# A list schedule that charges a change of tile shape on the tensor engine and keeps to the shape at hand for a while

## The chip, the cores and the metric

One core of one Trainium2 chip runs the whole program. The engines that matter are PE (TensorE, matrix products), ACT (ScalarE), DVE (VectorE), POOL (GpSimd) and SP, whose queue issues the DMAs that bring weights from DRAM to the on-chip SBUF. Products accumulate in eight PSUM banks. The metric is device time in microseconds (us), lower is better.

## The reference

256 tokens of 1024 features go through three residual blocks, each a mixer and a feed-forward part with layer norms:

```python
x = layer_norm(ALPHA * x + mix, ...)                 # layer 0: NSA attention + pooling
x = layer_norm(ALPHA * x + sqrelu_mlp(x, w1, w2))    # 1024 -> 4096 -> 1024
...                                                  # layer 1: gated linear attention, the same MLP
# block 2: mixer = gated delta rule (8 heads of 128, chunks of 64) + spatial gating unit,
#          then a hierarchical mixture of 16 experts (4 groups of 4, width 256, top 2 in the group)
a_mat = tril(k_beta @ k.T * decay, -1) + eye         # one 64x64 matrix for each chunk and head
u, w  = solve(a_mat, v_beta), solve(a_mat, k_beta * exp(g_cum))
for chunk in chunks:                                 # 4 of them, one after the other
    v_new = u - w @ state
    out   = q_dec @ state + qk @ v_new
    state = state * g_last + k_dec.T @ v_new
```

All inputs and the output are float32. The products need more than float16 accuracy.

## The kernel before

A weight arrives as float32 by DMA and is split into two float16 parts, the high part on ACT and the rest on DVE. A large product is then three float16 products (high by high, high by low, low by high). Nearly all the work on PE is of this kind: a 128x128 stationary tile (128 rows, 128 columns) and 256 or 512 moving columns. These are called dense here.

The delta rule (`mixer`, L1306) is different. For each token tile `solve` (L1371) inverts the 64x64 matrices of four heads and two chunks by doubling: `quads` (L1376) issues a batch of 8 float32 products with 64x64 stationary tiles in two corners of the array, five levels one after the other, with a DVE subtraction, an ACT copy and a POOL product between (L1443 to L1456). `own` (L1382) and `recur` (L1464) are further batches with 128x64, 64x64 or 64x128 stationary tiles. This chain has long waits in it, and the dense products of the same block that do not depend on it (projections, the spatial gating unit, the gates `pg`, the products `psu` and `py`) fill them. When the chain is done, `to_xt` (L740) transposes its result with the identity (`ptr`, 16 transposes of 128x128 in four groups, one group for each half of a token tile); ACT and DVE split each group into two float16 parts (L736), and the last `py` products (weight w_dn_out) use them. Then follow w_out, the router, and the experts: tokens are gathered with products of dense shape, and the up products of the experts have 128x64 stationary tiles (`peg`).

What sets the order is the class `Plan`. Every instruction is recorded with its inputs (`add`, L182) and a planned duration (`_cost`, L153). `order` (L228) then runs a list schedule: when an engine comes free in planned time, it takes the ready instruction with the lowest number in the program whose tiles have a place (L423 to L438). Results reach another engine after a planned delay. For PE two rules come first: if its recent activity is low, a large product is preferred (L405 to L414), and if the next product in the program uses other columns of the array, it goes along with the first (L415 to L421). Where PE has nothing to do, a filler goes out: a product of the constant k_ones with itself, to keep PE active (L484 to L497, issued at L546). The result is one fixed instruction list for each engine, issued at L551, so almost every row of the profile bears that line. On the chip every engine works through its list in order, and an instruction waits for its inputs. The planned durations decide the order only. SP's list of DMAs is in the same plan: a load goes out when the SBUF block that it fills has been released by its last reader.

In the order rows below, P_110 to P_117 are PSUM banks, H_n are blocks of the SBUF heap, and k_... are constants.

Of the kernel before, what the change touches and what calls it, by code (L numbers as in the profile page):

```python
# [8 lines left out]
F32 = mybir.dt.float32  # L9
# [15 lines left out]
class Plan:  # L25
    """Records engine instructions in program order and issues them in the order of a
    list schedule: per engine, the earliest recorded instruction whose inputs and tile
    slots are available goes first. Tiles of one tag take their slots in program order."""
# [8 lines left out]
    # the tensor engine runs at half its clock after a tick with less work than BUSY (ns at the full clock)  # L37
    TICK, BUSY = 10240 / 3, 1280.0

    # function tables of the scalar engine: those that hold a function, and what a change costs  # L40
    TABLES = {AF.Exp: (0,), AF.Tanh: (0, 10), AF.Gelu: (10,), AF.Ln: (5,)}
    LOAD = 1283.0

# [11 lines left out]
    def __init__(self, nc):  # L55
# [17 lines left out]
        self.low = 0.0  # L73
        self.keep, self.calm, self.leak, self.cap = None, 100.0, 0.55, 350.0
# [8 lines left out]
    def tile(self, shape, name, dtype, tag, slots, psum=False, lead=None):  # L83
        """slots: a count, or the numbers of the slots that the tile may take; None for a tile in the heap,
        in blocks of 1, 2 or 4 KB per partition. lead: a kind of tile that is filled well ahead of its use, while
        fewer of the kind than its quota are in the heap; kinds of one line take their places in program order."""
# [4 lines left out]
        if slots is None:  # L91
            self.units[handle.name] = next(k for k in (1, 2, 4) if size <= 1024 * k)
            slots = 0
# [9 lines left out]
    def branch(self, flag, bound, body):  # L103
        """The body runs if the integer in flag is above bound."""
        self.flags.append((flag, bound))
        self.segment += 1
        body()
        self.segment += 1
# [34 lines left out]
    @staticmethod  # L143
    def _run(ap, first):
        """Bytes of the longest run of consecutive addresses, the dimensions before first left out."""
        n = 1
        for step, count in reversed([d for d in ap.ap[first:] if d[1] > 1]):
            if step != n:
                break
            n *= count  # L150
        return n * mybir.dt.size(ap.dtype)
# [30 lines left out]
    def add(self, eng, method, fn, args, kwargs):  # L182
# [36 lines left out]
        cols = 0  # L219
        if eng == "PE":  # L220
            p0 = outs[0].offset // outs[0].ap[0][0]
            cols = sum(1 << b for b in range(p0 // 32, -(-(p0 + outs[0].ap[0][1]) // 32)))
# [3 lines left out]
                         eng == "PE" and ins[0].dtype == F32, table, self.urgent))  # L226

    def order(self):  # L228
# [50 lines left out]
        issued, warm, prior = 0, 0, -1  # L279
        since = level = last = 0.0  # L280
# [19 lines left out]
        def fit(t):  # L300
# [24 lines left out]
            if b > cur:  # L325
                # what the program needs from here to there, one instruction after the other, has to fit beside it
# [11 lines left out]
            # the place in the block that leaves the larger piece whole  # L338
# [46 lines left out]
        while issued < n:  # L385
# [10 lines left out]
            while moved:  # L396
                moved = False
                for e in ready:
# [16 lines left out]
                    if e == "PE" and pick is None and prior >= 0 and ops[prior + 1:prior + 2]:  # L415
                        # the second of two products in different columns of the array runs along with the first
# [5 lines left out]
                    late = None  # L422
                    while pick is None and ready[e] and len(skipped) < 48:  # L423
# [26 lines left out]
                    if e == "PE":  # L450
                        c = ops[pick][11]
                        prior = pick
                        clock()
                        if c & array:
# [6 lines left out]
                        if not fast:  # L461
                            dur *= 2
                    self.began[pick] = now
# [20 lines left out]
            if self.keep and busy["PE"] <= now and pe_left[seg] and seg % 2 == 0 and any(x[1] < 2 for x in events):  # L484
# [4 lines left out]
                elif level < 0 and free["P"] and self.began.get(self.keep[1], 1e9) + 500 < now:  # L489
# [3 lines left out]
                    flow(53.0)  # L493
                    array = 15
# [68 lines left out]
def block_kernel(ctx: ExitStack, tc: tile.TileContext, I: dict, out: bass.AP, dbg=None, stop=None):  # L563
# [59 lines left out]
    def tok(ap, k, ts):  # L623
        """Feature tiles k of the tokens ts (all or one of the two token tiles)."""
# [4 lines left out]
    def by_tile(ap):  # L629
        """The tokens as two tiles."""  # L630
# [13 lines left out]
    def load_unit(srcs, kt, n, name):  # L644
        """srcs: (rows by columns in DRAM, first column in the unit)."""
# [66 lines left out]
    def chunkB(us, xt, banks, name, halves=False, cols=(0, 128, 256, 384)):  # L712
        """512 output features of both token tiles; yields (psum view, feature tiles, tokens)."""
# [15 lines left out]
    def new_xt(name, kt=8, alloc=None, tiles=True):  # L729
        """tiles: each token tile in one piece, for readers that want one of them."""  # L730
# [28 lines left out]
    def norm_stats(y, eps):  # L759
        """The mean of each row and the inverse of its deviation."""  # L760
# [144 lines left out]
    # ================= layer 0 : NSA + pooling =================  # L905
    def nsa_layer(x, xt):
# [37 lines left out]
        # queries and keys times 16 in two float16 parts: both parts of a query over the partitions, each part of a key twice  # L944
# [32 lines left out]
        # compressed keys and values  # L977
        kch, kcl = (sm([128, 2, 16], nm, F16, bufs=1) for nm in ("kch", "kcl"))
        vc = sm([16, 2, 64], "vc", bufs=1)
        for c in range(2):  # L980
# [14 lines left out]
            # gelu by its tanh form, carrying a factor of 2  # L995
# [20 lines left out]
        # attention: rows of queries, softmax over keys, probabilities carry gate / denominator  # L1016
# [77 lines left out]
        # pooling  # L1094
# [29 lines left out]
    # ================= layer 1 : gated linear attention =================  # L1124
    def gla_layer(x, xt):
        def parts(t, shape, name):
            """Two float16 parts."""
# [29 lines left out]
        # gate path  # L1157
# [31 lines left out]
        # q and k with the running decays  # L1189
# [8 lines left out]
        # intra-chunk scores, keys back to token rows  # L1198
# [15 lines left out]
        # states  # L1214
# [19 lines left out]
        # outputs  # L1234
# [43 lines left out]
    # ================= block 2 mixer : gated delta rule and spatial gating =================  # L1278
    def mixer(x, xt, then=None):
# [31 lines left out]
        # decays  # L1311
# [26 lines left out]
        # projections, causal convolution, silu (carrying a factor of 2)  # L1338
# [32 lines left out]
        def solve(hg, i, qT, kT, vT):  # L1371
            """Within chunks; the matrices of the two chunks of a token tile lie one below the other."""
# [91 lines left out]
        def recur(hg):  # L1464
            # recurrence over chunks
# [71 lines left out]
        # spatial gating unit  # L1537
# [67 lines left out]
        # output gate of the delta rule, both branches summed  # L1605
# [20 lines left out]
    # ================= hierarchical mixture of experts =================  # L1626
    def moe():
# [6 lines left out]
        # the router takes the rows before their normalisation: (y - mean) * rs * g + b times w is  # L1634
        # rs * (y (g w) - mean * sum of (g w)) + sum of (b w)
# [18 lines left out]
        def route(i, y, gb, eps, name):  # L1654
# [18 lines left out]
            # the rank of each logit among its four; of equal ones the first counts as larger  # L1673
# [11 lines left out]
            # tokens of each expert, numbered from 1 in token order; 0 where a token is not the expert's  # L1685
# [31 lines left out]
            # weights of the two experts  # L1717
# [29 lines left out]
    def experts(x, xs, pm, cb, G16, flag):  # L1747
# [3 lines left out]
        # rows of the tokens gathered into 64 slots for each expert  # L1751
        def gather(a, b, f16):
            """For the pairs of experts from a to b."""
# [20 lines left out]
            # the way back, and the weight of each slot  # L1774
# [18 lines left out]
        def split(t, name):  # L1793
            """The weights in t, scaled, as two float16 parts."""
# [6 lines left out]
        def load_up(q, f16):  # L1801
            """By feature tile and expert, the gate's columns and the others."""
# [27 lines left out]
        def products(po, lhs, rhs, first, last):  # L1830
            """Accumulates in float32, or in float16 parts without the product of the two low ones."""
# [56 lines left out]
        # tokens beyond an expert's 64 slots, if any, go through every expert with their weights, zero for the others  # L1888
# [62 lines left out]
    def constants():  # L1951
# [18 lines left out]
        # for the matrices of one chunk: [row in the chunk, column]  # L1970
# [22 lines left out]
        # transposed first level: row 2r, column 2r + 1  # L1993
# [71 lines left out]
```

## Time and profile before

| | us |
|---|---|
| median of three timed runs | 1051.18 |
| lowest and highest | 1049.72, 1051.41 |
| span of the profiled execution | 1050.0 |
| PE busy in it | 1017.8 (97%) |
| DVE, ACT, POOL busy | 814.2, 581.6, 90.4 |

The page gives the profiled execution by its span; the median of the timed runs is 1.2 us above that. The stages, by the times at which their tiles are first or last written, are: attention and pooling to about 112, MLP to 282, gated linear attention to 389, MLP to 560, the first projections of the mixer to 613.5, delta rule with the spatial gating beside it to 781.6 (its last product), dense products of the gates and branches to 864.0 (first product of w_dn_out), those to 885.0, w_out and router to 924.7, experts to 1050.

### The profile page before, as it was taken

What the parts mean: (1) busy time and instruction counts of PE and PEld (TensorE: products, weight loads), DVE (VectorE), ACT (ScalarE), POOL (GpSimd) and SP (SyncE); (2) the same over time, 40 slices, a digit from 0 to 9 for tenths busy, and PEclk for the clock granted to TensorE, in tenths of its full rate; (3) what the DMA queues carried; (4) which work ended last, traced back from release to release, by engine and by line L of the source; (5) the groups of instructions that cost most, each with busy time, mean ns of one, the idle gap of its engine ahead of it and who ended that gap; (6) DMA issues with size and microseconds to landing.
All of it is one profiled execution on the core that took longest, in us unless ns stands there. A gap on an engine that the chain in (4) does not pass through costs nothing. (4 is left out here: it accounts for less than half of the span.)

```text
span 1050.0 us, 22081 instructions
## 1 busy us (share of the span) xinstructions
PE 1017.8 (97%) x8629; PEld 687.8 (66%) x8629; DVE 814.2 (78%) x1642; ACT 581.6 (55%) x1178; POOL 90.4 (9%) x129
## 2 busy tenths in 40 slices
PE   9998999999999999999999999999999999999994
PEld 8864767667457457666765876776678887653331
DVE  7898985656869887656579998785895759889874
ACT  7795564646466645645555543234454656467770
POOL 3003000000000100000001232020310000100000
PEclk9998999999999999999999999999999999899997
DMA  9947786575462467667985960421468467549991
GB/s 285 321 153 242 252 293 207 181 259 181 162 221 81 145 221 243 189 218 167 211 205 145 202 156 30 90 66 42 128 155 276 167 218 254 171 148 365 362 361 51
DMA packets 138913, 205.34 MB, mean 196 GB/s; under 512 B 23745, under 2 KB 59425, under 8 KB 138802
## 3 DMA queue, kind: packets, MB, share of 16 engines
q1 hardware_dynamic: 138802, 203.87, 63.2%
q8 instruction: 69, 1.13, 0.4%
q14 instruction: 42, 0.34, 0.1%
HBM read 202.79 MB, written 1.05 MB: 194 GB/s over the span
## 5 line engine op out<-in xcount | busy, mean ns | idle before, releaser
L551 PE MATMUL P<-H,H 128*128 128x256 f16 (+9 forms) x7480 | 940.8, 296 | 7.9 <-issue 3.3
L551 PEld LDWEIGHTS <-H 128*128 128x128 f16 (+2 forms) x6416 | 548.3, 99 | 267.2 <-issue 40.0
L551 ACT ACTIVATE H<-H 128x512 f16<-128x512 f32 (+2 forms) x777 | 443.7, 621 | 198.9 <-PE P L551 110.6
L551 DVE SCALAR_TENSOR_TENSOR H<-H,H 128x512 f16<-128x512 f32 (+2 forms) x715 | 460.3, 690 | 66.4 <-ACT H L551 64.5
L551 ACT ACTIVATE H<-P 128x512 f32<-128x512 f32 (+7 forms) x247 | 120.5, 500 | 228.8 <-PE P L551 217.1
L551 PEld LDWEIGHTS P<-H,H 64*64 64x64 f32 (+3 forms) x1232 | 69.0, 140 | 43.5 <-issue 23.4
L551 DVE TENSOR_TENSOR H<-H 128x512 f32<-128x512 f32 (+2 forms) x49 | 34.2, 697 | 48.2 <-ACT H L551 48.1
L551 POOL TENSOR_TENSOR s_bnr<-s_bnr,k_mhalf 128x1 f32<-128x1 f32 x14 | 13.4, 960 | 594.3 <-DVE s_bnr L551 594.3
L551 DVE SCALAR_TENSOR_TENSOR H<-P,H 128x512 f32<-128x512 f32 (+2 forms) x56 | 37.9, 685 | 22.3 <-ACT H L551 11.1
L551 PE MATMUL P<-k_ident,H 128*128 128x128 f32 x257 | 45.7, 286 | 6.8 <-DVE H L551 4.8
L551 PEld LDWEIGHTS P<-k_ident,H 128*128 128x128 f32 x257 | 31.1, 144 | 19.2 <-DVE H L551 10.5
L551 DVE TENSOR_TENSOR H<-H,P 128x512 f32<-128x512 f32 (+1 forms) x32 | 19.7, 617 | 27.6 <-PE P L551 27.3
L551 DVE TENSOR_TENSOR H<-H,H 128x512 f16<-128x512 f32 (+5 forms) x37 | 26.3, 713 | 8.4 <-ACT H L551 7.8
L551 DVE SCALAR_TENSOR_TENSOR H<-P,s_cw,H 128x254 f32<-128x254 f32 (+2 forms) x72 | 29.8, 471 | 0.0
L551 PE MATMUL P<-H 64*64 64x64 f32 (+5 forms) x312 | 26.7, 244 | 0.0
L551 DVE TENSOR_TENSOR H<-P,H 128x512 f16<-128x512 f32 (+2 forms) x38 | 23.6, 640 | 3.3 <-ACT H L551 3.3
L551 DVE SCALAR_TENSOR_TENSOR H<-H,P 128x512 f32<-128x512 f32 (+1 forms) x24 | 14.3, 594 | 12.2 <-ACT H L551 9.5
L546 PE MATMUL P<-k_ones 128*128 128x128 f16 x197 | 19.0, 262 | 1.1 <-DVE k_ones L551 1.1
L551 DVE SCALAR_TENSOR_TENSOR H<-H,s_bnr,H 128x512 f32<-128x512 f32 x28 | 20.0, 744 | 0.0
L551 DVE SCALAR_TENSOR_TENSOR H<-H,s_bnm,H 128x512 f32<-128x512 f32 x28 | 19.8, 742 | 0.0
L551 DVE BATCH_NORM_STATS2 s_bns<-H 128x6 f32<-128x512 f32 x28 | 19.0, 684 | 0.3
L546 PEld LDWEIGHTS <-k_ones 128*128 128x128 f16 x197 | 16.8, 123 | 3.1 <-issue 1.2
(221 smaller groups left out, 361.3 us busy)
## 6 DMA issues: line engine op xcount, KB each, us to landing
H<-in_mlp_w_dram SPq DMA_DIRECT2D x128, 512.0 KB, 4.7
H<-in_w_in_dram SPq DMA_DIRECT2D x64, 512.0 KB, 5.9
H<-in_expert_w_gate_dram SPq DMA_DIRECT2D x64, 256.0 KB, 5.9
H<-in_expert_w_up_dram SPq DMA_DIRECT2D x64, 256.0 KB, 5.9
H<-in_expert_w_down_dram SPq DMA_DIRECT2D x32, 512.0 KB, 7.1
H<-in_c_w_in_dram SPq DMA_DIRECT2D x24, 512.0 KB, 4.4
H<-in_a_w_in_dram SPq DMA_DIRECT2D x12, 512.0 KB, 8.3
H<-in_a_w_out_dram SPq DMA_DIRECT2D x8, 512.0 KB, 11.2
```

Of the source, the lines that this page charges most:

```text
L546: tc.nc.tensor.matmul(self.phys["P", ~i][:, 0:128], ap, ap, start=True, stop=True)
L551: fn(*[self._place(a) if isinstance(a, bass.AP) else a for a in args], **{k: self._place(a) if isinstance(a, bass.AP) else a for k, a in k ...
```

## The change

It is made in the plan alone; no instruction of the kernel is added or altered apart from the number of fillers. Each PE instruction is given a mode: rows and columns of its stationary tile, each rounded up to 32, 64 or 128. The plan keeps the mode at hand. A product of another mode gets 105 ns more planned duration (`TURN`), and so does a filler that follows another mode. And when PE comes free, after the two older rules, up to eight of the lowest-numbered ready products of the mode at hand are tried first, as long as products of another mode have been ready for less than 2000 ns (`stay`). After that the old rule picks. Comments are removed in many places, which is not shown.

```diff
+    TURN = 105.0
...
+        self.stay = 2000.0
...
-        cols = 0
+        cols, mode = 0, None
         if eng == "PE":
+            mode = tuple(next(k for k in (32, 64, 128) if n <= k) for n in (ins[0].shape[0], self._free(ins[0])))
...
+        shape, self.turns, since_other = (128, 128), 0, 1e18
...
                     late = None
+                    if e == "PE" and pick is None and ready[e]:
+
+                        same = sorted(x for x in ready[e] if ops[x[1]][15] == shape)[:8]
+                        if any(ops[x[1]][15] != shape for x in ready[e]):
+                            since_other = min(since_other, now)
+                        else:
+                            since_other = 1e18
+                        limit = self.stay
+                        if now - since_other < limit:
+                            for top in same:
+                                if take(top[1]):
+                                    pick = top[1]
+                                    ready[e].remove(top)
+                                    heapq.heapify(ready[e])
+                                    break
                     while pick is None and ready[e] and len(skipped) < 48:
...
+                        turn = self.TURN if ops[pick][15] != shape else 0.0
+                        if turn:
+                            since_other = 1e18
+                        shape = ops[pick][15]
+                        self.turns += turn > 0
...
                         if not fast:
                             dur *= 2
+                        dur += turn
...
                     dur = 56.0 if fast else 107.0
...
+                    if shape != (128, 128):
+                        dur += self.TURN
+                        shape = (128, 128)
```

Counted in the two instruction lists of PE, a change of mode between neighbours occurs 450 times before and 233 times after. By stage:

| stage | before | after |
|---|---|---|
| attention and pooling | 42 | 36 |
| gated linear attention | 34 | 26 |
| delta rule and spatial gating, from the first pG to the first w_out product | 290 | 123 |
| w_out and router | 4 | 4 |
| experts | 80 | 44 |

Of the 290 and 123, the delta rule's stage up to its last product has 229 and 81. The two MLPs have none. The fillers are 197 before and 179 after. The code has moved down by 30 lines, so L551 is L581 and L546 is L576 in the order of the changed kernel.

The solver of the delta rule on PE: P_111 and P_113 get batches of 64x64 products, P_116 is filled by dense products of a projection. Before:

```order
L551 LDWEIGHTS H_79
L551 MATMUL P_116<-H_94,H_79 128x256
L551 MATMUL P_113<-H_109,H_106 64x64 x3
L551 LDWEIGHTS H_98
L551 MATMUL P_116<-H_94,H_98 128x256
L551 MATMUL P_113<-H_109,H_106 64x64 x2
L551 MATMUL P_111<-H_100,H_108 64x64 x2
L551 LDWEIGHTS H_98
L551 MATMUL P_116<-H_63,H_98 128x256
L551 MATMUL P_111<-H_100,H_108 64x64 x2
```

The same level of the solver in the changed list, two whole batches in a row with dense products before and after:

```order
L581 LDWEIGHTS H_69
L581 MATMUL P_116<-H_95,H_69 128x256
L581 MATMUL P_111<-H_75,H_107 64x64 x8
L581 MATMUL P_111<-H_107,H_75 64x64 x8
L581 LDWEIGHTS H_80
L581 MATMUL P_116<-H_95,H_80 128x256
```

The next batch of 64x64 products stands 21 dense products further on. Before, one dense product stood between every two to four small ones.

The transposes of the delta branch (k_ident) on PE, ahead of the first product of w_dn_out. Before, three of the four groups stand about 1,360 rows earlier, and the last one stands here between dense products:

```order
L551 LDWEIGHTS H_85
L551 MATMUL P_117<-H_94,H_85 128x256
L551 MATMUL P_112<-k_ident_128,H_65 128x128 x4
L551 LDWEIGHTS H_93
L551 MATMUL P_116<-H_106,H_93 128x256
```

After, all four groups stand together, and eleven more fillers (k_ones) like the first follow before the product that needs them:

```order
L581 LDWEIGHTS H_69
L581 MATMUL P_116<-H_95,H_69 128x256
L581 MATMUL P_111<-k_ident_128,H_76 128x128 x4
L581 MATMUL P_110<-k_ident_128,H_76 128x128 x4
L581 MATMUL P_112<-k_ident_128,H_91 128x128 x4
L581 MATMUL P_113<-k_ident_128,H_91 128x128 x4
L576 LDWEIGHTS k_ones_139
L576 MATMUL P_115<-k_ones_139 128x128
```

All four groups moved to the end of the other dense work of the mixer, with the fillers where nothing else was ready.

The start of the experts on PE: P_114 gets the up products (64 columns stationary, shown as 64x512), the other banks the gathering. Before:

```order
L551 LDWEIGHTS H_90
L551 MATMUL P_115<-H_73,H_90 128x512
L551 LDWEIGHTS H_73
L551 MATMUL P_115<-H_68,H_73 128x512
L551 LDWEIGHTS H_89
L551 MATMUL P_114<-H_96,H_89 64x512
L551 LDWEIGHTS H_89
L551 MATMUL P_114<-H_86,H_89 64x512
L551 LDWEIGHTS H_90
L551 MATMUL P_110<-H_73,H_90 128x512
```

After, 18 more up products like the last two follow directly:

```order
L581 LDWEIGHTS H_99
L581 MATMUL P_115<-H_79,H_99 128x512
L581 LDWEIGHTS H_79
L581 MATMUL P_115<-H_68,H_79 128x512
L581 LDWEIGHTS H_93
L581 MATMUL P_114<-H_98,H_93 64x512
L581 LDWEIGHTS H_93
L581 MATMUL P_114<-H_65,H_93 64x512
```

Twenty up products now run before the rest of the gathering; before, it was two.

## Rows read from the trace of the kernel before

**Rows 1.** The page: span and busy time of each engine (share, instructions).

```profile
span 1050.0 us, 22081 instructions
PE 1017.8 (97%) x8629; PEld 687.8 (66%) x8629; DVE 814.2 (78%) x1642; ACT 581.6 (55%) x1178; POOL 90.4 (9%) x129
```

**Rows 2.** Busy time of each engine by stage; the columns stand in its first line.

```profile
core 0: us, PE busy (x) PEld busy (x) DVE busy (x) ACT busy (x) POOL busy (x), PEclk, DMA share, GB/s
20.00:112.00 92.00, 85.72 (x780) 59.34 (x778) 83.41 (x261) 68.95 (x176) 12.57 (x11) 0.96 0.71 228
...
560.00:613.50 53.50, 53.50 (x444) 39.30 (x442) 51.59 (x108) 27.46 (x52) 11.32 (x7) 1.00 0.76 177
613.50:781.60 168.10, 164.69 (x1960) 116.98 (x1960) 131.65 (x296) 63.55 (x183) 38.18 (x41) 0.99 0.34 89
781.60:864.00 82.40, 82.40 (x741) 72.27 (x738) 53.75 (x90) 47.05 (x92) 1.01 (x1) 1.00 0.66 222
864.00:885.00 21.00, 21.00 (x195) 18.83 (x193) 20.11 (x34) 16.72 (x32) 0.00 (x0) 1.00 0.74 234
...
931.80:1025.60 93.80, 91.91 (x631) 36.01 (x629) 80.13 (x139) 68.65 (x132) 0.00 (x0) 1.00 1.04 348
```

**Rows 3.** The same columns for a dense stretch and one of the solver.

```profile
582.10:613.20 31.10, 31.10 (x288) 27.87 (x285) 30.71 (x65) 14.99 (x28) 4.56 (x3) 1.00 0.79 176
639.80:645.20 5.40, 5.40 (x67) 3.45 (x65) 5.07 (x8) 3.35 (x5) 1.00 (x1) 1.00 0.00 1
```

**Rows 4.** PE products by form in that stretch of the solver: count, busy, mean ns.

```profile
L551 PE MATMUL P<-H,H 64*64 64x64 f32 x56 | 4.0, 236 | 0.0
L551 PE MATMUL P<-H,H 128*128 128x256 f16 x11 | 3.1, 283 | 0.0
```

**Rows 5.** Weight loads there in order: start, length, operation, tile, form, count.

```profile
641.02 0.10 PEld L551 LDWEIGHTS <-H 128*128 128x128 f16 x1
641.23 0.20 PEld L551 LDWEIGHTS P<-H,H 64*64 64x64 f32 x4
641.49 0.10 PEld L551 LDWEIGHTS <-H 128*128 128x128 f16 x1
...
642.45 0.10 PEld L551 LDWEIGHTS <-H 128*128 128x128 f16 x1
642.66 0.31 PEld L551 LDWEIGHTS P<-H,H 64*64 64x64 f32 x8
643.04 0.10 PEld L551 LDWEIGHTS <-H 128*128 128x128 f16 x1
```

**Rows 6.** What PE waited for from 613.5 to 885: total, times, longest.

```profile
PEld P L551 <- DVE H L551: 6.7, 15, 1.6
...
PE P L551 <- DVE H L551: 3.4, 5, 1.4
```

**Rows 7.** The last transposes of the delta branch, read by ScalarE and VectorE.

```profile
863.76 1.09 ACT L551 ACTIVATE H<-P 128x512 f32<-128x512 f32 x2 [0.60 <-PE P L551]
...
864.88 0.69 DVE L551 TENSOR_TENSOR H<-P,H 128x512 f16<-128x512 f32 x1 [0.91 <-ACT H L551]
```

**Rows 8.** Start of the experts on PE, and on the DMA queue of SP.

```profile
924.69 0.11 PEld L551 LDWEIGHTS <-H 128*64 128x64 f16 x2 [0.42 <-issue]
...
931.33 1.27 PE L551 MATMUL P<-H,H 128*64 128x512 f16 x10
...
931.80 0.37 SPq L551 DMA_DIRECT2D H<-in_expert_w_gate_dram  x1
...
934.05 0.46 SPq L551 DMA_DIRECT2D H<-in_expert_w_up_dram  x1
```

**Rows 9.** What that queue waited for from 911 to 936: total, times, longest.

```profile
SPq L551 <- PE P L551: 22.0, 2, 21.1
```

**Rows 10.** Loads of the experts by the page: count, KB each, us to landing.

```profile
H<-in_expert_w_gate_dram SPq DMA_DIRECT2D x64, 256.0 KB, 5.9
```

**Rows 11.** A stretch at half clock in the mixer, columns as in rows 2.

```profile
628.20:631.50 3.30, 3.30 (x28) 2.13 (x25) 3.30 (x11) 0.00 (x0) 2.89 (x5) 0.50 0.39 117
```

More of the change, by code (lines that the diff above doesn't have):

```diff
@@ L225, in add @@
         self.ops.append((eng, fn, args, kwargs, dur, xfer, preds, firsts, tiles, me + self.shift, self.segment, cols,
-                         eng == "PE" and ins[0].dtype == F32, table, self.urgent))
+                         eng == "PE" and ins[0].dtype == F32, table, self.urgent, mode))
     def order(self):
```

## The prediction

> **What bounds the kernel now.** I read the page first, then a table by stage, then the order of weight loads in one stretch of the solver, then the waits. The page shows PE busy for 97% of a span of 1050.0 us [rows 1]; the reader is to see that the time can fall in two ways only: PE gets less to do, or a late stage bound by something else ends sooner. The table shows where PE is the limit. It is busy 53.50 of 53.50, 82.40 of 82.40 and 21.00 of 21.00 us in the mixer's dense parts, and 164.69 of 168.10 us in the delta rule [rows 2]. From 931.80 to 1025.60 the DMA engines are at a share of 1.04 with 348 GB/s: there the loads set the pace, whatever PE does [rows 2]. A busy PE is not a PE at its peak, so the next view counts products: the dense stretch has 288 in 31.10 us, 0.108 us each, and DVE is busy for 30.71 us of it without holding PE back; the solver's stretch has only 67 in 5.40 us [rows 3], 56 of them 64x64 and 11 dense [rows 4]. The loads show why. A dense load and four small ones alternate, and from one dense load to the next pass 0.47 us (641.02 to 641.49); with eight small ones it is 0.59 us (642.45 to 643.04) [rows 5].
>
> **The price of one change of shape.** Four more small products cost 0.59 - 0.47 = 0.12 us, so 0.030 us each. A dense one costs 0.108. The period of 0.47 holds one dense, four small and two changes: (0.47 - 0.108 - 0.12) / 2 = 0.121 us. Over the whole stretch, where each of 11 dense products stands alone and makes two changes: (5.40 - 11 x 0.108 - 56 x 0.030) / 22 = (5.40 - 1.19 - 1.68) / 22 = 0.115 us. I take 0.115, since it averages 22 changes. The ends are 0.10 (small products at 0.036) and 0.123 (at 0.027).
>
> [...] The trace says 0.115, and the sum goes by the trace.
>
> **The change, part by part.** It removes no product. It reorders all five instruction lists, and the changes of mode fall from 450 to 233.
>
> Delta rule and spatial gating, 290 to 123: 167 x 0.115 = -19.2 us, all on PE, which is the limit there. Ends: -16.7 (0.10) and -20.5 (0.123). For this the other engines have to keep up. From 613.5 to 885.0 DVE is busy for 131.65 + 53.75 + 20.11 = 205.5 us of 271.5, 76% [rows 2]; in 271.5 - 19.2 = 252.3 us that is 81%. The first projections ran at 96% (51.59 of 53.50) with PE full, attention at 91% [rows 2]. So there is cover, of some 25 us at 91%.
>
> Waits at the heads of batches. PE works in order, so a batch whose input is late holds every product behind it, and ACT and DVE behind those. Before, PE lost 6.7 us in 15 waits ahead of a load and 3.4 us in 5 ahead of a product, both for DVE [rows 6]; of 168.10 us PE was idle for 3.4 [rows 2]. There are now about 61 heads (half of 123 changes) in place of 145. A dense run of up to 2 us ahead of a batch gives its inputs time beyond their planned readiness, which speaks for fewer waits; the second batch of a pair, following directly, has no such time, which speaks for more. Ends: -3.4 (all idle time goes) and +6 (the 6.7 us come once more, nearly); I take +1, near the middle.
>
> The chain itself is started later by up to 2 us at a step. Its end stands with 9 x 48 = 432 dense products of the mixer still behind it in the new list, 432 x 0.108 = 47 us; before it was 82.4 us [rows 2]. So it may slip by 47 us before PE runs dry: cost 0.
>
> The transposes of the delta branch. Before, only the last group stood alone ahead of its readers, and dense products ran beside its split. From the ACT read at 863.76 to the end of the DVE subtraction (864.88 + 0.69) are 1.8 us [rows 7], with dense products as cover. Now four groups stand together, followed by 12 fillers, two dense products and 11 more fillers: the cover is gone. The first reader needs both halves' first features, three groups: 3 x 0.55 on ACT, then 0.69 on DVE, 2.3 us, and about 0.2 to hand over from PE: +2.5 us. Ends 0 (the groups are split while dense products still run) and +4 (four in series on DVE).
>
> Gated linear attention, 34 to 26: 8 x 0.115 = -0.9 us, at PE's price. Attention, 42 to 36: PE is not full there (85.72 of 92.00, DVE 83.41 [rows 2]) and waits on others; six changes come to 0.7 us, which I take as 0, with ends -2.5 and +3 because its order moves too. The two MLPs keep their products and have no changes: 0. W_out and router: 4 changes in both, 0.
>
> Experts, 80 to 44. At PE's price it would be 36 x 0.115 = 4.1 us, but the loads set the pace. What counts is when they start. SP's queue waits 21.1 us for a PE release [rows 9] and issues at 931.80, in the middle of the up products from 931.33 on; the first two of these ran at 924.69, gathering came between [rows 8]. In the new list 20 follow directly, at 1.27 / 10 = 0.12 us each, so the block is released some 5 us earlier. Four loads stand from 931.80 to 934.05 [rows 8], of 256 KB each [rows 10]; the next ones depend on later releases. 1.05 MB at 348 GB/s is 3.0 us: -3.0. Ends: -5 (all later loads follow too) and +2 (the gathering is delayed, and with it the second group of products).
>
> Sum: -19.2 + 1 + 2.5 - 0.9 + 0 - 3.0 = -19.6 us. The span becomes 1030.4; with the 1.2 us between the span and the median of the runs shown it is 1031.6. With all ends in the good sense it is about 1021, with all in the other some 1048.
>
> **Rivals.**
>
> VectorE becomes the limit of the delta rule. By the new list 240 dense products (26 us) move into this stage, and with them their share of DVE work, 26 x 53.75 / 82.40 = 17 us. Of the 167 changes 148 go from this stage, 17.0 us. It would last 168.1 - 17.0 + 26 = 177 us with 149 us of DVE, 84%. For it: DVE now does 131.65 of 168.10, 78%, and the solver's steps on it are part of a chain. Against it: 96% in the stage before. If it can't exceed 78%, the stage takes 191 us, 14 more: 1045.
>
> [...]
>
> [...]
>
> Slower: waits at the heads of batches take the gain's place. The planned times are too early for DVE's and POOL's results in the chain, and with 61 in-order heads PE stands at each. It decides at 20.6 us (the gain of the sum without its +1): 0.34 us at each head on average; at 0.5 us it is 30 us and 1061. For it: the 15 waits before took 0.45 us each [rows 6]. Against it: 15 waits among some 145 heads, and the dense run ahead of each.
>
> It doesn't do what it says: the gap at a change is the hand-over of batches rather than of shape, and stays with the batches. Then about 1050. Against it: 0.47 us recur with equal products on both sides, with nothing waited for [rows 5].
>
> **How the numbers follow.** Forecast 0.68, VectorE 0.10, clock 0.06, higher price 0.05, slower 0.07, no effect 0.04. A measurement of this kernel tells about 0.2%, 2.1 us, from no change. Faster: the forecast, VectorE, clock and higher price, 0.89, less 0.02 for mixtures of them that end near 1050: 0.87. Within 0.2%: 0.05. Slower: 0.08. The range goes from 1022 (the higher price) to 1042; it leaves out the slower case, no effect and most of VectorE, 0.19 together.
>
> **What would show it.** Right: from the first pG to the first w_out product 271.5 us become about 255; a dense run and a batch alternate with periods near 21 x 0.108 + 16 x 0.030 + 2 x 0.115 us; the first loads of the experts go out some 5 us sooner after the first up product; about 2.5 us idle or filled ahead of w_dn_out. Wrong: PE waits on DVE of more than 20 us in the mixer, granted clock of 0.50 in more than two stretches of it, a mixer that keeps its 271 us with 167 changes fewer, or experts whose last load doesn't land about 3 us sooner after their first up product.

## The result, and the profile after

The changed kernel takes 1040.86 us (1039.5 to 1042.42, 4 runs) against 1050.45 us before in the same runs: a ratio of 0.9916, interval 0.9895 to 0.9937. It is faster by 9.6 us. The forecast was 1031.6, a gain of 19.6 us, so about half of it came.

The page of the profiled execution, span and busy times of the engines, answers to [rows 1]:

```profile
span 1039.5 us, 22053 instructions
PE 994.9 (96%) x8611; PEld 683.7 (66%) x8611; DVE 811.8 (78%) x1642; ACT 579.4 (56%) x1178; POOL 90.3 (9%) x129
```

The table by stage, with the columns of [rows 2]. The cuts are at the same products as there: the mixer from the first pG to the first w_out product (613.5 to 885.0 before) is now 614.8 to 877.6.

```profile
20.00:113.20 93.20, 86.84 (x743) 59.22 (x744) 86.17 (x267) 68.93 (x175) 12.69 (x11) 0.93 0.77 245
...
561.30:614.80 53.50, 53.50 (x445) 39.09 (x443) 51.62 (x106) 27.48 (x52) 11.33 (x7) 1.00 0.74 174
614.80:877.60 262.80, 251.15 (x2919) 206.21 (x2919) 202.88 (x418) 124.74 (x304) 38.56 (x42) 0.98 0.49 144
877.60:913.60 36.00, 32.90 (x223) 19.47 (x223) 34.53 (x93) 16.73 (x32) 6.44 (x5) 1.00 0.61 199
913.60:1015.00 101.40, 95.26 (x665) 40.75 (x666) 85.89 (x164) 73.15 (x141) 1.16 (x1) 0.98 0.96 322
```

The mixer lasts 262.8 us in place of 271.5. PE's busy time in it fell from 268.09 (the sum over the three rows of [rows 2]) to 251.15, by 16.9 us, but its idle time rose from 3.4 to 11.65. What PE waited for there, total, times and longest, answers to [rows 6]:

```profile
PE P L581 <- DVE H L581: 10.6, 10, 2.2
...
PEld P L581 <- DVE H L581: 9.1, 14, 2.5
```

And the half clock (a granted clock of 0.50), before in one stretch of 3.3 us of the mixer [rows 11], now stands in two, of 3.3 and 6.8 us. Attention has two stretches of 6.8 us in place of one (the new one from 42.7), the experts have one of 3.2 us that they had not before, and in the router there was one before, of which nothing is left. Windows with the columns of rows 2, first four of after, then one of before:

```profile
42.70:49.50 6.80, 6.42 (x66) 5.33 (x67) 6.27 (x47) 5.36 (x27) 0.00 (x0) 0.50 1.05 387
629.90:633.20 3.30, 3.30 (x24) 2.24 (x23) 2.94 (x10) 0.00 (x0) 1.79 (x3) 0.50 0.90 204
745.80:752.60 6.80, 6.80 (x90) 5.63 (x87) 4.61 (x8) 2.72 (x6) 0.00 (x0) 0.50 1.03 158
967.80:971.00 3.20, 3.20 (x11) 0.90 (x11) 3.20 (x7) 2.43 (x5) 0.00 (x0) 0.50 1.02 366
```

```profile
911.50:921.60 10.10, 10.10 (x72) 9.14 (x70) 6.20 (x22) 1.23 (x2) 2.09 (x2) 0.50 0.31 113
```

The solver itself looks as forecast. Weight loads in order, as in [rows 5]:

```profile
668.27 1.01 PEld L581 LDWEIGHTS P<-H,H 64*64 64x64 f32 x32 [0.21 <-issue]
669.35 2.19 PEld L581 LDWEIGHTS <-H 128*128 128x128 f16 x21
671.75 1.01 PEld L581 LDWEIGHTS P<-H,H 64*64 64x64 f32 x32 [0.21 <-issue]
```

One period is 671.75 - 668.27 = 3.48 us; 21 x 0.108 + 32 x 0.030 + 2 x 0.115 is 3.46. (The prediction's sign had 16 x 0.030. A row of the trace counts passes, and here a float32 product has two: the two batches of 8 products in the list are x32 in these rows.) But here and there a batch stands and waits. PE at one of these places, and VectorE just ahead of it:

```profile
741.76 0.82 PE L581 MATMUL P<-H,H 128*128 128x256 f16 x6
744.75 1.33 PE L581 MATMUL P<-H,H 64*64 64x64 f32 x36 [2.17 <-DVE H L581]
```

```profile
741.15 0.16 DVE L581 TENSOR_TENSOR s_onm<-s_onm,s_hp 128x4 f32<-128x4 f32 x1 [0.90 <-POOL s_onm L581]
741.23 1.66 DVE L581 SCALAR_TENSOR_TENSOR H<-H,s_onm,H 128x128 f32<-128x128 f32 x6
742.81 1.29 DVE L581 SCALAR_TENSOR_TENSOR H<-H,H 128x512 f16<-128x512 f32 x2
744.01 0.68 DVE L581 TENSOR_TENSOR H<-H,P 128x512 f32<-128x512 f32 x1
```

The last of these is the solver's subtraction that PE waits for. The operations ahead of it in VectorE's list are no part of that chain: the gating of the branch's output, and two splits of weights that are needed much later. VectorE worked through them without a pause, after it had itself stood for 0.90 us for POOL, so the subtraction was late because VectorE was behind. The half-clock stretch begins at 745.8, after the wait and within the small products that follow it; which of the two it goes with is taken up at the kernel with the lighter VectorE.

The ledger, from span 1050.0 to 1039.5 (10.5 us), one execution of each kernel: attention and what follows up to the mixer +1.3, mixer -8.7, w_out and router -3.7 (39.7 to 36.0, the half-clock stretch of 10.1 us gone), experts and end +0.6.

### The profile page after: what moved, and what is told of

The parts are those of the page before. It is cut to its first block, busy times and chain, and to the rows that moved or that the text cites. A ratio compares the mean times of both kernels' runs of the same rounds, so it can differ in the third digit from the quotient of the medians.

```text
span 1039.5 us, 22053 instructions
## 1 busy us (share of the span) xinstructions
PE 994.9 (96%) x8611; PEld 683.7 (66%) x8611; DVE 811.8 (78%) x1642; ACT 579.4 (56%) x1178; POOL 90.3 (9%) x129
## 5 line engine op out<-in xcount | busy, mean ns | idle before, releaser
L581 PE MATMUL P<-H,H 128*128 128x256 f16 (+10 forms) x7664 | 932.8, 294 | 20.1 <-DVE H L581 12.8
L581 PEld LDWEIGHTS <-H 128*128 128x128 f16 (+2 forms) x6416 | 552.9, 99 | 268.7 <-issue 37.1
L581 ACT ACTIVATE H<-H 128x512 f16<-128x512 f32 (+2 forms) x777 | 444.1, 621 | 229.5 <-DVE H L581 114.0
L581 DVE SCALAR_TENSOR_TENSOR H<-H,H 128x512 f16<-128x512 f32 (+2 forms) x715 | 459.6, 689 | 72.1 <-ACT H L581 68.7
L581 ACT ACTIVATE H<-P 128x512 f32<-128x512 f32 (+7 forms) x247 | 119.3, 498 | 189.4 <-PE P L581 184.7
L581 PEld LDWEIGHTS P<-H,H 64*64 64x64 f32 (+3 forms) x1416 | 72.2, 144 | 40.6 <-issue 28.3
L581 DVE TENSOR_TENSOR H<-H 128x512 f32<-128x512 f32 (+2 forms) x49 | 34.2, 699 | 49.5 <-ACT H L581 49.4
L581 POOL TENSOR_TENSOR s_bnr<-s_bnr,k_mhalf 128x1 f32<-128x1 f32 x14 | 13.9, 990 | 529.6 <-DVE s_bnr L581 518.1
L581 DVE SCALAR_TENSOR_TENSOR H<-P,H 128x512 f32<-128x512 f32 (+2 forms) x56 | 37.8, 686 | 22.5 <-ACT H L581 11.3
L581 PE MATMUL P<-k_ident,H 128*128 128x128 f32 x257 | 46.6, 282 | 5.8 <-DVE H L581 4.2
L581 PEld LDWEIGHTS P<-k_ident,H 128*128 128x128 f32 x257 | 31.6, 143 | 18.6 <-DVE H L581 9.3
L581 DVE TENSOR_TENSOR H<-H,P 128x512 f32<-128x512 f32 (+1 forms) x32 | 19.6, 616 | 17.4 <-PE P L581 17.3
L581 DVE TENSOR_TENSOR H<-H,H 128x512 f16<-128x512 f32 (+5 forms) x37 | 25.8, 700 | 6.4 <-ACT H L581 6.2
L581 DVE SCALAR_TENSOR_TENSOR H<-P,s_cw,H 128x254 f32<-128x254 f32 (+2 forms) x72 | 30.0, 472 | 0.0
L581 DVE TENSOR_TENSOR H<-P,H 128x512 f16<-128x512 f32 (+2 forms) x38 | 23.4, 642 | 2.7 <-ACT H L581 2.4
L581 DVE SCALAR_TENSOR_TENSOR H<-H,s_bnr,H 128x512 f32<-128x512 f32 x28 | 20.7, 767 | 0.5 <-POOL s_bnr L581 0.5
L581 DVE BATCH_NORM_STATS2 s_bns<-H 128x6 f32<-128x512 f32 x28 | 19.0, 686 | 2.6 <-ACT H L581 2.3
L581 DVE SCALAR_TENSOR_TENSOR H<-H,s_bnm,H 128x512 f32<-128x512 f32 x28 | 20.3, 757 | 0.0
L581 PE MATMUL P<-H 128*64 128x64 f32 (+4 forms) x128 | 15.9, 268 | 1.4 <-DVE H L581 1.2
L576 PE MATMUL P<-k_ones 128*128 128x128 f16 x179 | 15.5, 238 | 1.2 <-DVE k_ones L581 1.1
L581 DVE SCALAR_TENSOR_TENSOR H<-H,P 128x512 f32<-128x512 f32 (+1 forms) x24 | 14.2, 593 | 2.1 <-PE P L581 1.6
L576 PEld LDWEIGHTS <-k_ones 128*128 128x128 f16 x179 | 13.2, 109 | 3.1 <-issue 1.1
```

What stands on the lines that cost most here:

```text
L576: tc.nc.tensor.matmul(self.phys["P", ~i][:, 0:128], ap, ap, start=True, stop=True)
L581: fn(*[self._place(a) if isinstance(a, bass.AP) else a for a in args], **{k: self._place(a) if isinstance(a, bass.AP) else a for k, a in k ...
```

## The experiments

Theory A was that the waits show because VectorE is late against the plan while PE keeps to it; theory B that keeping to a shape makes them by itself; theory C that the price upsets the plan's measure of PE activity; theory D, formed after eight runs, names why VectorE is late, and E is its rival, that charging a change at all costs time by what it does to the order. All times below have the kernel before on the same chip beside them (1049.1 to 1050.2 us).

**The rule without the price.**

```diff
-    TURN = 105.0
+    TURN = 0.001
```

> The new rule with a change of shape priced at nothing (TURN 0.001 ns, enough for the rule's own bookkeeping): 121 changes in the mixer as against 123, 240 in all. Theory A (the waits at batch heads show because the plan now prices the changes, so PE runs on its planned time while DVE's results come late; before, PE itself was late against the plan by the unpriced changes and so met results that were there): PE again runs late by about 121 x 0.115 = 14 us over the mixer, the waits of the mixer fall back from 7.6 us towards 3, no stretch at half clock follows one, and the time is 1031 to 1036. Theory B (the waits come from keeping to a shape, because the second batch of a pair follows the first directly, whatever the plan's prices are): waits as in the changed kernel, 1039 to 1043.

Measured 1031.2 us, ratio 0.9822 (0.9801 to 0.9844): almost 10 us faster than the changed kernel with as many changes of shape. The mixer's window and PE's waits for VectorE in it (the profiled execution, at 1036.55 us, was the longest of the five):

```profile
619.10:870.60 251.50, 246.69 (x2921) 202.50 (x2921) 203.03 (x419) 125.17 (x303) 39.21 (x42) 0.99 0.51 154
```

```profile
PE P L581 <- DVE H L581: 2.5, 5, 1.4
...
PEld P L581 <- DVE H L581: 5.1, 10, 1.6
```

251.5 us is 20.0 less than before, the gain of the changes as forecast; PE is idle for 4.8 us in place of 11.65. The rule does not make the waits by itself, so B falls; they come with the price.

**The price without the rule.**

```diff
-        self.stay = 2000.0
+        self.stay = 0.0
```

> The price alone (TURN 105, stay 0): by its order the mixer has 744 changes of shape, 454 more than the kernel before, with the same products. If a change costs 0.115 us wherever it stands: 454 x 0.115 = 52 us more than before, mixer about 320 us, time 1095 to 1105. If the gap belongs to the hand-over of batches and not to the shape: within 10 us of the kernel before, 1045 to 1060.

Measured 1146.28 us, ratio 1.0904 (1.0874 to 1.0934); the mixer takes 350.7 us, 79.2 more than before for 454 more changes, 0.174 us each. That is outside both ranges. The gap goes with the changes of shape and not with the batches, and my 0.115 was too little here. The loads show why:

```profile
650.85 0.19 PEld L581 LDWEIGHTS P<-H,H 64*64 64x64 f32 x2 [0.21 <-issue]
651.10 0.11 PEld L581 LDWEIGHTS <-H 128*128 128x128 f16 x2
651.43 0.19 PEld L581 LDWEIGHTS P<-H,H 64*64 64x64 f32 x2 [0.21 <-issue]
```

A visit is now one product (two passes), not a pair (four passes, as in [rows 5]). Its period of 0.58 us less two dense products leaves 0.36 us, as much as a visit of a pair left (0.47 - 0.108): the second product of a pair had come nearly free, and pairs are split. The change as made needs the rule to repair what its own price does to the order.

**Shorter and longer stay.** In the second kernel the number is 4000.0.

```diff
-        self.stay = 2000.0
+        self.stay = 1000.0
```

> Products of another shape wait 1000 ns at most in place of 2000: 145 changes in the mixer, 22 more than the changed kernel, 2.5 us at 0.115. Theory A: waits about as in the changed kernel, so 1041 to 1045. Theory B: fewer direct pairs of batches, waits smaller by some 3 us, which outweighs the changes: 1037 to 1041.

> Products of another shape wait up to 4000 ns: 109 changes in the mixer, 14 fewer than the changed kernel, but the chain of the delta rule ends later, with fewer dense products behind it. If only the number of changes counts: 1.6 us less, 1037 to 1041. If the chain can be held back too long: PE runs out of dense products beside it, some 16 us more waits in the mixer, 1053 to 1062 (theories A and B both expect this).

Measured 1045.09 us, ratio 0.9944 (0.9923 to 0.9964), and 1049.24 us, ratio 0.9993 (0.9978 to 1.0008). The first is 0.1 us above theory A's range, but PE's waits for VectorE ahead of a product are 6.8 us in its mixer, not 10.6 as A would have them. The second is a miss: its mixer takes 259.2 us, 3.6 less than the changed kernel's, so the chain was not held back too long there. It lost 8 us before the mixer began (622.7 against 614.8) and 10 in w_out and router (45.9 against 36.0 us). What of that is the rule and what the clock, I did not separate.

**VectorE's work made lighter, the lists kept.** The edit is where the instructions are issued, after the order is made; LIGHT holds the beginnings of the names of the mixer's weight parts; a counter in the edit is not shown. This kernel leaves out the low parts of these weights.

```diff
                 if self.ops[i][10] == seg:
+                    if self.ops[i][0] == "DVE" and kwargs.get("scalar") == WS and kwargs["out"].tensor.name.startswith(LIGHT):
+                        tc.nc.vector.tensor_scalar(self._place(kwargs["out"]), self._place(kwargs["in1"]), 1.0 / 8192.0, None, op0=OP.mult)
+                        continue
```

> The changed kernel's own lists on all engines, except that for 144 pieces of the mixer's weights the low float16 part is not computed: VectorE writes the high part times 1/8192 in one cheap operation instead of scale-and-subtract (this leaves the low-part products wrong in value, the same in number). [...] Theory A (VectorE's results reach the batch heads late because VectorE is behind with other work while PE keeps to the plan): waits of PE for VectorE in the mixer from 20 us by the view of waits to under 8, no half-clock stretch after one, mixer 262.9 to about 253, time 1029 to 1033. Theory C (the planned price upsets the order itself, batches cut short and the chain set back): the order is the same, so mixer within 3 us of 262.9 and time 1037 to 1041.

Measured 1027.33 us, ratio 0.9784 (0.9764 to 0.9804), 1.7 us below A's range. The mixer's window and waits:

```profile
615.40:864.80 249.40, 245.82 (x2920) 203.04 (x2920) 164.77 (x415) 122.56 (x302) 35.58 (x42) 1.00 0.48 144
```

```profile
PE P L587 <- DVE H L587: 3.5, 6, 1.3
...
PEld P L587 <- DVE H L587: 2.5, 7, 0.7
```

With PE's list unchanged, 38 us less of work on VectorE takes 13.4 us from the mixer, and its mean granted clock there is 1.00 where the changed kernel's was 0.98. So the waits came from VectorE's load ahead of the chain's operations, and the order of PE's own products is good enough for 249 us. C expected 259.9 or more here.

The lists being the same, one place can be set beside the other: the 80 small passes at 744.75 of the changed kernel, and below them the same 80 here.

```profile
744.75 3.68 PEld L581 LDWEIGHTS P<-H,H 64*64 64x64 f32 x80 [2.45 <-DVE H L581]
```

```profile
734.87 2.52 PEld L587 LDWEIGHTS P<-H,H 64*64 64x64 f32 x80 [0.21 <-DVE H L584]
```

With the long wait ahead of them the granted clock fell from 1.00 to 0.50, 1.0 us into them: the first 32 took 0.92 us, 0.029 each, the other 48 took 2.75 us, 0.057 each. With 0.21 us ahead of them all 80 took 2.52 us, 0.032 each. Nor did a long wait do it by itself: one of 2.13 us ahead of a batch at 650.70 of the changed kernel, with dense products behind its first 16 passes, was followed by no half clock (granted 1.00 from 633.2 to 745.8). That is one case of each, so that wait and small passes together lower the clock is not shown. The router shows what is chance: with these same lists its half-clock stretch is back (10.1 us from 890.8 on), and w_out and router take 39.6 us against 36.0.

**The price without its effect on the activity measure.**

```diff
                         self.turns += turn > 0
+                        level += self.leak * turn
+                        seen += 0.375 * turn
```

> The changed kernel with the price of 105 ns kept, but the time of a change no longer lowers the plan's measure of PE activity, by which a dense product is preferred when activity is low. 125 changes in the mixer, planned mixer 258.5 as against 259.7. Theory C (the price costs time because it drives that measure under its limit and so breaks batches and forces dense products ahead of the chain): the mixer falls to about that of the unpriced plan, time 1031 to 1035. Theory A (what costs is that PE is planned exactly and has no lateness of its own to hide late results): waits as in the changed kernel, 1038 to 1042.

Measured 1044.99 us, ratio 0.9955 (0.9940 to 0.9969), mixer 266.3 us. C falls: without that effect it is no better. It is also 3 us above A's range.

**VectorE's results planned 1 us later.**

```diff
-        ("DVE", "PE"): 230, ("DVE", "ACT"): 130, ("DVE", "DVE"): 127, ("DVE", "POOL"): 160,
+        ("DVE", "PE"): 1000 + 230, ("DVE", "ACT"): 130, ("DVE", "DVE"): 127, ("DVE", "POOL"): 160,
```

> The changed kernel with the planned way from VectorE to PE 1000 ns longer, so that a batch is put in PE's list about 1 us later than its inputs by the plan. 131 changes in the mixer; the chain's end moves 27 us back in the plan. Theory A: PE waits for VectorE less, total waits in the mixer from 7.6 to about 3 us and no half-clock stretch, time 1033 to 1038. Theory C, and equally a chain that has become too long by the 1 us at each step: 1040 to 1048.

Measured 1043.81 us, ratio 0.9958 (0.9933 to 0.9984), mixer 261.3 us, waits of PE ahead of a product for VectorE 8.6 us, 10 times. This is in C's range and failed for A as I had put it. Room at every hand-over makes the planned chain longer, and that VectorE's list puts still more ahead of it would be a reason; it is not shown.

**Theory D.** Why is VectorE late? The plan gives a pair of 64x64 products 109 + 56 = 165 ns; four passes took 0.12 us [rows 5]. So the plan's price for a small product held part of the change, and the charge of 105 ns counts that part twice. The relieved kernel shows that the plan was too slow: it ran its mixer in 249.4 us where the plan had 259.7. A plan that believes PE slow would give VectorE more splits ahead of the chain's operations than there is time for. Counted in the lists: ahead of the subtraction at 744.01 above, an early one of the second half of the heads, VectorE has 76 splits of the mixer's weights before, 102 after, 84 in the unpriced kernel. This count is not the whole of it: with a stay of 1000 it is 82, and without the activity effect 87, and their mixers take 264.4 and 266.3 us. So a price of a small product that holds no change should bring back the gain with the charge in place.

```diff
-                return (1.705 * n if n >= 128 else 216.0 if self._free(ins[0]) > 64 else 109.0), 1.667 * n * ins[0].shape[0] / 128
+                return (1.705 * n if n >= 128 else 216.0 if self._free(ins[0]) > 64 else 64.0), 1.667 * n * ins[0].shape[0] / 128
```

> The changed kernel with its price of 105 ns and its rule, and with the planned duration of a 64x64 product (64 moving columns, float32) at 64 ns in place of 109; its twin stays at 56. Four passes, which is such a pair, took 0.12 us in the kernel before, and the plan gave them 165 ns, so a charge for the change came on top of a price that already held part of it. 106 changes in the mixer; the chain ends 146 us after its start in the plan as against 188. Theory D (theory A made exact: PE is planned too slow, so the other engines' lists put more splits ahead of the chain's operations than fit, and VectorE is late at batch heads): waits of 0.4 us and more in the mixer from 12 us to under 6, mixer 246 to 252, time 1027 to 1033. Rival E (charging a change at all costs time by what it does to the order): as the changed kernel, 1038 to 1044.

Measured 1031.29 us, ratio 0.9832 (0.9812 to 0.9852). 81 splits stand ahead of that subtraction. Window and waits:

```profile
614.80:864.90 250.10, 244.66 (x2916) 202.30 (x2916) 204.85 (x419) 123.36 (x301) 37.37 (x42) 1.00 0.52 155
```

```profile
PE P L581 <- DVE H L581: 5.1, 7, 1.3
...
PEld P L581 <- DVE H L581: 6.2, 12, 1.6
```

The charge of 105 ns and the rule are there, and the mixer is 12.7 us shorter, with PE idle for 5.4 us of it. So the double charge is what cost the gain, and E falls as its reason. What goes with the waits over the kernels is how long the plan takes the mixer to be, read from the same lists as the counts. Planned at 242 to 243 us (before, unpriced, 64 ns), PE is idle in it for 3.4 to 5.4 us; at 253.0 (half the price, below) for 8.3; at 258.5 to 261.6 (changed, without the activity effect, stay of 1000) for 8.3 to 12.0; at 267.8 and 275.9 (VectorE planned later, stay of 4000) for 10.7 and 10.0. The price without the rule, planned at 342.0 and measured at 350.7, has 6.0: there PE is as slow as the plan has it. That the splits are the link from the plan's length to the waits is argued, not shown.

**That one number alone, in the kernel before.** The edit is the last one above, made in the kernel before.

> The kernel before, with neither price nor rule, and only the planned duration of a 64x64 product at 64 ns in place of 109. By its order the mixer has 158 changes in place of 290: the list schedule alone then keeps pairs and batches together. At 0.115 us a change 15 us less; with up to 4 us more of waits the time is 1034 to 1040. If the number of changes does not decide: 1046 to 1052.

Measured 1032.25 us, ratio 0.9840 (0.9821 to 0.9859), 1.8 us below its range, mixer 251.8 us with 158 changes. Neither the price nor the rule is needed for most of the gain; one planned duration, set to what the trace shows, gives some 18 us, nearly twice what the change gave.

**Half the price.**

```diff
-    TURN = 105.0
+    TURN = 50.0
```

> The changed kernel with a price of 50 ns in place of 105: 132 changes in the mixer, planned mixer 253.0 as against 259.7 and 243.4 unpriced. Theory D: waits between those of the unpriced and of the changed kernel, time 1033 to 1039. Rival E: any price upsets the order as much, 1039 to 1044.

Measured 1040.95 us, ratio 0.9922 (0.9900 to 0.9944). Its mixer lies between, as D has it (251.5 unpriced, 258.4 at 50 ns, 262.8 at 105), but the total is outside D's range and within E's. W_out and router take 39.8 us there against 36.0, with a half-clock stretch of some 10 us that the changed kernel happens not to have; without these 3.8 us it would be in D's range. By the total alone this run does not tell D from E.

**The unpriced rule in the mixer alone, and with the small product at 64 ns.** Both have TURN at 0.001 besides; the numbers are those of the mixer's instructions in the program.

```diff
-                        limit = self.stay
+                        limit = self.stay if 5805 <= min(ready[e])[1] < 9389 else -1.0
```

> The new rule unpriced, and only where the lowest-numbered ready product of PE belongs to the delta rule and spatial gating; attention, gated linear attention and experts are ordered as before. 121 changes in the mixer, 277 in all. The unpriced rule everywhere lost 3.9 us in attention and 1.6 from there to the mixer, against the kernel before. If those losses come from the rule in attention and the mixer's gain of 19.9 us is its own: 1026 to 1029. If the losses are chance in the clock's half-speed stretches: 1028 to 1034.

> The unpriced rule in the mixer alone, with the 64x64 product planned at 64 ns: 99 changes in the mixer, the chain's end 138 us after its start in the plan. At 0.115 us a change 2.5 us less than with the rule in the mixer alone at 109 ns; with the chain's end earlier, fewer dense products are needed behind it. Theory D expects 1024 to 1029. If unpriced changes let PE fall behind and nothing else matters: the same as that kernel, within 2 us.

Measured 1028.63 us, ratio 0.9824 (0.9801 to 0.9846), and 1025.57 us, ratio 0.9776 (0.9756 to 0.9795). The first is in both of its ranges, so whether the unpriced rule's losses ahead of the mixer were its own or the clock's stays open; its five runs go from 1026.71 to 1034.34 us as the mean granted clock goes from 0.992 to 0.982. The second is in D's range, and the fastest kernel of the study that computes all of the reference: 24.6 us below the kernel before, 15.3 below the changed one. Its mixer:

```profile
612.90:857.90 245.00, 242.28 (x2926) 201.56 (x2925) 198.91 (x411) 123.65 (x300) 37.43 (x42) 1.00 0.51 152
```

It still beats the priced kernel with 64 ns by 5 us in the mixer. Whether the charge itself costs that, or the last few changes (99 against 106), these runs do not tell apart.

## Why half of the predicted gain came

- **The price of a change** (0.115 us, 167 of them, -19.2): right, and a little low. PE's busy time in the mixer fell by 16.9 us although the half clock cost it some 3.5 us more there and the fillers of the bubble below 1.3, so 21.7 without these, 0.13 us a change. (The 3.5 is an estimate, half of the 10.1 us of its two stretches, 5.1, less half of the 3.3 us before, 1.65, from the small passes of 0.057 us at the half clock and 0.029 ahead of it.) The unpriced kernel says the same: 21.4 us less busy time (268.09 to 246.69) for 169 changes. No run shows the higher price behind the forecast's 0.05 and its 1022; the runs showed this 0.13 us a change, and 0.174 us where the price without the rule split the pairs.
- **Waits at the heads of batches** (+1, ends -3.4 and +6): this is the step that failed, with the experts' term below as the next. It measured +11.7: 8.2 us more of idle PE, and 3.5 us of half clock. I argued that up to 2 us of dense products ahead of a batch gives its inputs time. That holds on PE, but I looked at PE's list alone: VectorE's list had been laid out by the same plan, for a mixer of 259.7 us, and it was late; with VectorE's work lighter on the same lists, PE's idle time in the mixer is 3.6 us. The wait of 2.17 us at 744.75 has a dense run ahead of it and is there all the same.
- **VectorE's cover** (96% in the stage before): true and beside the point. VectorE is busy for 202.88 of 262.80 us, 77%; over the mixer it was not short of time, but where PE waited it was behind. My rival of a VectorE that cannot exceed 78% had the delta rule's stage at 191 us, and 191.5 it was, at 79%:

```profile
614.80:806.30 191.50, 179.85 (x2256) 142.14 (x2255) 150.49 (x329) 79.09 (x214) 37.55 (x41) 0.97 0.40 109
```

  It is no bound all the same. In the kernel with 64 ns the same stage takes 154.2 us with VectorE busy for 89% of it:

```profile
614.80:769.00 154.20, 148.76 (x2037) 117.16 (x2036) 137.71 (x308) 65.64 (x191) 36.37 (x41) 1.00 0.43 112
```

- **The chain itself** (0): right. From its last product at 806.3 to the transposes at 853.65 PE has 47 us of dense products, and no wait.
- **The bubble at the transposes** (+2.5, ends 0 and +4): 1.3. After the 16 transposes the fillers run from 855.40 to 856.07 and from 856.29 to 856.91, 0.67 + 0.62 us:

```profile
853.65 1.91 PE L581 MATMUL P<-k_ident,H 128*128 128x128 f32 x16
855.40 0.83 PE L576 MATMUL P<-k_ones 128*128 128x128 f16 x12
856.07 0.38 PE L581 MATMUL P<-H,H 128*128 128x256 f16 x2
856.29 0.78 PE L576 MATMUL P<-k_ones 128*128 128x128 f16 x11
856.91 1.80 PE L581 MATMUL P<-H,H 128*128 128x256 f16 x15
```

- **Experts** (-3.0): +0.6. The first loads did go out early, 2.9 us after the first up product in place of 7.1, but only two of them; then SP's queue stood again, for PE (4.8 us), until 922.17, because the next blocks are released by products that had moved behind the gathering. I had taken four. It came out as one of the prediction's signs of being wrong: the last loads are issued 91.0 us after the first up product (913.56 to 1004.61), 90.6 before (924.69 to 1015.24). SP's queue, as in [rows 8]:

```profile
916.44 0.37 SPq L581 DMA_DIRECT2D H<-in_expert_w_gate_dram  x1
916.86 0.47 SPq L581 DMA_DIRECT2D H<-in_expert_w_up_dram  x1
922.17 0.37 SPq L581 DMA_DIRECT2D H<-in_expert_w_gate_dram  x1
```

- **Attention and gated linear attention** (0 and -0.9): +1.3 together, with a new half-clock stretch of 6.8 us in attention; what it cost was not separated. **Router** (0): -3.7, the half-clock stretch gone. That is luck: the stretch is back in the half-priced order (some 10 us), and in the relieved kernel (10.1 us) with the very lists of the changed one. With it the changed kernel would have gained some 6 us.
- **The rivals.** The slower one named the mechanism that took half of the gain, at 0.19 us a head (11.7 / 61) where it needed 0.34 to turn the sign. The clock, which the forecast gave 0.06, had a part as well: the mixer had two half-clock stretches where it had one, and the longer one, of 6.8 us, came where a wait of 2.17 us and a run of 80 small passes stood together.
- **The ends.** "All ends in the good sense" leaves out attention's -2.5, which the other end (+3) has in it: it is 1019, not 1021. Nothing hangs on it.

## What to carry to other kernels

When a scheduler's cost table gets a new term, look for what its older terms already hold: here the small product had been priced with its change of shape in it, and charging the change again made the plan believe PE slow. The damage need not be on the engine with the wrong price: here VectorE was the one that came late. So compare the length that the plan gives a stage with what the trace gives it, and read a changed order on all engines; PE's list alone did not show these waits.

## What of the hardware was not expected

A pair of 64x64 products in two corners of the array, visited between dense products, took 0.36 us with both changes of shape; a single one took 0.36 us as well (0.58 less two dense products). And a single wait of 2.17 us of PE ahead of 80 small passes was followed, 1.0 us after it ended, by 6.8 us at half clock (x90 in that window), while the same 80 passes after a wait of 0.21 us, and a wait of 2.13 us ahead of 16 passes and a dense run, were not.
